# A two-layer hybrid trunk step: scale loaded ahead of shift, decay rows by transposes, lighter vector work in mixer C

## Chip, cores and metric

The kernel runs on one core of one Trainium2 chip. The metric is the device time of one execution in microseconds; a kernel's time is the median of its runs. TensorE is the matrix engine (PE in the rows, with PEld for its weight loads), VectorE is DVE, ScalarE is ACT, GpSimd is POOL, and SP is the queue that issues all transfers here.

## What is computed

Two token streams, 128 context tokens and 256 latent tokens (384 columns together), pass through two layers of model width 1024. A layer first modulates a normalised input, mixes it in three ways side by side, merges the three, and then runs an MLP with squared ReLU. Cut to what matters here:

```python
def residual_block(x, mod, p, mixer):
    sh1, sc1, g1, sh2, sc2, g2 = jnp.split(mod, 6, axis=-1)
    y, extra = mixer(rmsnorm(x, p['norm1_g']) * (1 + sc1) + sh1)
    ...

# mixer C, per direction, head and chunk (gated delta rule)
gc = jnp.cumsum(gl, axis=-1)
decay = exp(gc[:, None] - gc[None, :]) where i >= j, else 0
a_mat = strict_lower((k * beta) @ k.T * decay)
t_mat = inverse(I + a_mat)
o = rmsnorm(o_forward + o_backward, c_onorm_g) * silu(c_z)
```

## The kernel before

Activations are held transposed: a tile is 128 channels by 384 tokens, eight tiles make the model width. A projection is made in three matmuls per 128x128 weight block (high weights by high and by low activations, low weights by high activations; `mm3`, L149 to L152), after a weight tile of 512 KB has been loaded into one of three `raw` buffers and split by ScalarE (high half, L146) and VectorE (low half, L147). The order of the instructions on each engine is chosen when the kernel is built, by a list scheduler that goes by priorities (`phase`, `stream`): the code is written as a "chain" and a "fill" that is worked in beside it, and the order doesn't change while the kernel runs.

Layer 0 begins with `lead()` (from L353). It computes the first two sixths of the modulation, shift and scale, from 8 MB of `w_ada`, in three parts (`PARTS`): part 0 loads the columns of both shift and scale for model blocks 0 to 3 as eight loads of 512 KB, parts 1 and 2 the columns for two blocks each as eight loads of 256 KB. In each part TensorE multiplies the conditioning vectors (the stationary operand, 32 columns wide, in four column groups) by the loaded columns (L155 with tile `mraw`), VectorE transposes the result and adds the bias (L400 to L404), and `modulated` (L217 to L230) makes the tiles hh and hl from `x`, scale, shift and the reciprocal norm `rb`. Between the parts, `advance` runs the projections of w_small and of three key tiles of w_in as far as hh and hl exist: the early projections, whose results wait in PSUM banks. From their banks mixer C's gates (tile `kab`, L556 to L560) and the convolution of the keys (L644 to L659) are made.

In layer 1 the modulation is ready beforehand. There w_small and two key tiles are projected from tiles that are only scaled (`scaled`, L232 to L244, the shift as two more columns), while the norm is computed; `normalised` (L546 to L554) then multiplies the result by the norm and adds the shift's two columns as a bias. All eight tiles of `modulated` are made ahead of it in the code.

Mixer C's chain: for each of three token tiles n and two directions d, the decay rows (tile `gr`, L811 to L833) are twelve bf16 matmuls in which a column of one of three pieces of the log decay, spread over 128 columns, multiplies a triangle of ones (`tri16`); a masking matmul `bar` is added (L825) and ScalarE takes the exponential. VectorE makes the matrices M and QK from them, then inverts the 32x32 diagonal blocks in 31 steps (L866 to L871), transposes the result (L873, L875), and `spread` (L940 to L946) writes it as block-diagonal tiles X0T and X0, four products with the mask `bd2` for each n. Small 64x64 matmuls p1 to p5 finish the inverse; `e1` (L948 to L952) evacuates the first of them, the lower halves on VectorE and the upper ones on ScalarE; `e3` (L959 to L962) applies a correction. Gates of mixer C (`gate`, L710 to L716) are made in the fill: silu(z) times the output gain in a tanh, a pass of VectorE for 0.5 t + 0.5 (L715), and a product with gain and z (L716). The last gating is a plain product (L1097).

## Time and profile before

| | |
|---|---|
| median of 3 runs | 1532.94 us (1529.35 to 1535.46) |
| profiled execution | 1534.62 us, span 1532.8 us |
| mean granted TensorE clock | 0.992 of full |
| TensorE busy | 1490.1 us, 97% of the span, 9694 matmuls |
| VectorE busy | 995.7 us, 65%, 2159 instructions |
| ScalarE busy | 768.6 us, 50%, 1523 instructions |
| moved by DMA | 212.82 MB, mean 139 GB/s |

The profiled execution is one run of its own, so its time differs a little from the median. A matmul's busy time overlaps that of the next one, so the distance from start to start tells what one costs. A wait in the view of the waits is idle time of an engine, put down to what came last.

### The profile page before, as it was taken

The numbers are of one execution on the slowest core, as the hardware profiler recorded it, in microseconds if no ns is written. First come the engines' busy times: TensorE is split into PE (matmuls) and PEld (weight loads), VectorE is DVE, ScalarE is ACT, GpSimd is POOL, SyncE is SP. The second block draws the span as 40 slices with busy tenths as digits, with TensorE's granted clock in tenths as the row PEclk, the third lists the DMA queues.
The fourth block names the chain that finished last, engine by engine and source line by source line (L and its number), as shares of the span: only waits on it lengthen the run. The fifth ranks groups of instructions, "written<-read, shape, count | busy, mean of one in ns | idle before, by whom it ended". The sixth has DMA issues, their size and how long they took to land.

```text
span 1532.8 us, 25235 instructions
## 1 busy us (share of the span) xinstructions
PE 1490.1 (97%) x9694; PEld 1372.9 (90%) x9694; DVE 995.7 (65%) x2159; ACT 768.6 (50%) x1523; POOL 22.4 (1%) x82
## 2 busy tenths in 40 slices
PE   5999999999999999999999999999999999999997
PEld 2898798977889999999998987889889999999997
DVE  4667895564446788888868778956645575553333
ACT  3466634455424666643335576344564456663222
POOL 0000200000000000000000002000000000000000
PEclk9999999999999999999999999999999999999999
DMA  9532131242688466677743331213324434444342
GB/s 316 165 108 86 51 101 56 76 143 89 210 280 270 144 190 197 200 242 241 248 142 113 97 96 54 85 57 106 99 75 138 128 121 124 124 124 127 122 128 77
DMA packets 80856, 212.82 MB, mean 139 GB/s; under 512 B 8800, under 2 KB 24544, under 8 KB 80608
## 3 DMA queue, kind: packets, MB, share of 16 engines
q1 hardware_dynamic: 80736, 211.21, 44.1%
q8 instruction: 76, 1.25, 0.3%
q14 instruction: 44, 0.36, 0.1%
HBM read 204.59 MB, written 4.75 MB: 137 GB/s over the span
## 4 chain that ended last, share of the span: by engine, by line
PE 73%; DVE 10%; issue 10%; DMA 3%; ACT 1%; POOL 1%; SPq 1%; DVEq 0%; POOLq 0%; ACTq 0%
PE g L152 19%; PE g L150 19%; PE g L151 19%; PE c L155 5%; PE f L155 3%; DVE wlo L147 2%; DMA araw<-in_w_ada_dram 2%; PE o L155 2%; DVE aacc L319 2%; PE f L455 1%; PE g L155 1%; DVE h L869 1%; DVE hl L239 1%; DVE blk L871 1%; PE c L150 1%
## 5 line engine op out<-in xcount | busy, mean ns | idle before, releaser
L146 ACT CAST whi<-raw 128x1024 fp32r<-128x1024 f32 x268 | 280.6, 1048 | 479.0 <-PE g L151 429.6
L152 PE MATMUL g<-hh,wlo 128*128 128x384 f32 (+1 forms) x1424 | 487.8, 344 | 6.0 <-DVE wlo L147 6.0
L150 PE MATMUL g<-hh,whi 128*128 128x384 f32 (+1 forms) x1424 | 488.3, 344 | 0.6 <-DVE gpiece L181 0.3
L151 PE MATMUL g<-hl,whi 128*128 128x384 f32 (+1 forms) x1424 | 486.8, 343 | 0.1
L147 DVE TENSOR_TENSOR wlo<-raw,whi 128x1024 fp32r<-128x1024 f32 x268 | 325.9, 1216 | 155.0 <-PE g L152 129.2
L152 PEld LDWEIGHTS g<-hh,wlo 128*128 128x128 f32 x1424 | 269.4, 189 | 15.4 <-DVE wlo L147 10.4
L150 PEld LDWEIGHTS g<-hh,whi 128*128 128x128 f32 x1424 | 269.5, 190 | 9.4 <-issue 6.5
L151 PEld LDWEIGHTS g<-hl,whi 128*128 128x128 f32 x1424 | 269.4, 189 | 6.9 <-issue 3.5
L152 PE MATMUL g<-fh,wlo 128*128 128x384 f32 x512 | 173.0, 338 | 1.0 <-DVE wlo L147 1.0
L150 PE MATMUL g<-fh,whi 128*128 128x384 f32 x512 | 173.4, 339 | 0.0
L151 PE MATMUL g<-fl,whi 128*128 128x384 f32 x512 | 172.6, 337 | 0.0
L319 DVE SCALAR_TENSOR_TENSOR aacc<-araw,cs,aacc 128x512 f32<-128x512 f32 x168 | 117.0, 745 | 13.9 <-DMA araw<-in_w_ada_dram 11.9
L152 PEld LDWEIGHTS g<-fh,wlo 128*128 128x128 f32 x512 | 96.0, 187 | 2.4 <-DVE wlo L147 2.3
L150 PEld LDWEIGHTS g<-fh,whi 128*128 128x128 f32 x512 | 96.0, 188 | 1.6 <-issue 1.6
L151 PEld LDWEIGHTS g<-fl,whi 128*128 128x128 f32 x512 | 96.0, 188 | 0.0
L150 PE MATMUL g<-brh,whi 128*128 128x384 f32 x192 | 65.9, 343 | 0.5 <-DVE gate L537 0.5
L436 ACT ACTIVATE at_p<-at_p,at_nm 128x384 f32<-128x384 f32 (+1 forms) x96 | 51.8, 541 | 28.8 <-DVE at_nm L433 27.8
L152 PE MATMUL g<-brh,wlo 128*128 128x384 f32 x192 | 65.9, 343 | 0.0
L151 PE MATMUL g<-brl,whi 128*128 128x384 f32 x192 | 65.1, 339 | 0.0
L147 DVE TENSOR_TENSOR fl<-fa,fh 128x384 fp32r<-128x384 f32 x64 | 35.5, 555 | 38.9 <-ACT fh L146 38.9
L347 DVE SCALAR_TENSOR_TENSOR x<-g,mod,x 128x128 f32<-128x128 f32 x64 | 23.7, 412 | 51.2 <-PE g L152 47.9
L1231 ACT ACTIVATE fa<-fa,fb 128x128 f32<-128x128 f32 (+1 forms) x128 | 51.1, 447 | 1.9 <-DVE fa L1229 1.9
(333 smaller groups left out, 1885.4 us busy)
## 6 DMA issues: line engine op xcount, KB each, us to landing
raw<-in_w_ff_dram SPq DMA_DIRECT2D x128, 512.0 KB, 3.8
raw<-in_w_in_dram SPq DMA_DIRECT2D x102, 512.0 KB, 3.6
araw<-in_w_ada_dram SPq DMA_DIRECT2D x96, 256.0 KB, 3.4
raw<-in_w_branch_dram SPq DMA_DIRECT2D x24, 512.0 KB, 3.7
araw<-in_w_ada_dram SPq DMA_DIRECT2D x24, 512.0 KB, 6.5
raw<-in_w_out_dram SPq DMA_DIRECT2D x16, 512.0 KB, 3.6
mraw<-in_w_ada_dram SPq DMA_DIRECT2D x8, 512.0 KB, 9.0
mraw<-in_w_ada_dram SPq DMA_DIRECT2D x16, 256.0 KB, 7.2
```

What stands on the lines that cost most here:

```text
L146: S.copy(hi, src)
L147: V.tensor_tensor(out=lo, in0=src, in1=hi.bitcast(F32), op=ALU.subtract)
L150: PE.matmul(ps, lhsT=wh, rhs=rh, start=start, stop=False)
L151: PE.matmul(ps, lhsT=wh, rhs=rl, start=False, stop=False)
L152: PE.matmul(ps, lhsT=wl, rhs=rh, start=False, stop=stop)
L155: return PE.matmul(ps, lhsT=lhsT, rhs=rhs, start=start, stop=stop)
L239: V.scalar_tensor_tensor(out=lo[:, c], in0=x[k][:, c], scalar=gp[:, k, s:s + 1], in1=hi[:, c].bitcast(F32), op0=ALU.mult, op1=ALU.subtract)
L319: V.scalar_tensor_tensor(out=acc[:, s, :], in0=raw, scalar=cs[:, k, s:s + 1], in1=acc[:, s, :], op0=ALU.mult, op1=ALU.add)
L347: V.scalar_tensor_tensor(out=x[k][:, c], in0=ps[:, c], scalar=m[:, b0 + k, s:s + 1], in1=x[k][:, c], op0=ALU.mult, op1=ALU.add)
L436: S.activation(sm[:, :nk], sm[:, :nk], AF.Exp, bias=nm[:, u:u + 1], scale=-1.0, accum_out=den[:, u:u + 1])
L455: PE.transpose(pt[:, j * P:(j + 1) * P], ps_[half, n][:, c * P:(c + 1) * P], ident)
L1231: S.activation(a[:, c], a[:, c], AF.Relu, bias=b[:, s:s + 1])
```

## The change

In layer 0, `lead()` loads `w_ada` in four parts of eight 256 KB loads: scale for blocks 0 to 3, scale for blocks 4 to 7, then shift in the same two halves. The early projections (now w_small and all four key tiles) use tiles that are only scaled, without norm and shift. When the shift is complete, a pass of TensorE with the shift as the stationary operand goes over all early weights and gives their bias (`shifted`, tile ebs); `normalised` multiplies by the norm and adds the bias. The tiles hh and hl for everything else are made from x times scale times norm (tile lt) plus shift. From part 1 on, a part's blocks begin with its last block row. Twelve staging buffers `mraw` serve all parts. In layer 1 kab is normalised after five of the eight modulated tiles. The decay rows become four f32 transposes of the cumulated decay. The gate keeps (t + 1) z, with the factor 0.5 and the gain moved to later steps. `spread` makes X0 on ScalarE, and `e1` copies on ScalarE alone.

```diff
-PARTS = ((4, 2), (2, 1), (2, 1))
+LOADS = (2, 1, 2, 0)
 ...
+    def scaled_tile(k, gp, hi, lo):
+        for s, c in STREAMS:
+            S.activation(hi[:, c], x[k][:, c], AF.Copy, scale=gp[:, k, s:s + 1])
+            V.scalar_tensor_tensor(out=lo[:, c], in0=x[k][:, c], scalar=gp[:, k, s:s + 1],
+                                   in1=hi[:, c].bitcast(F32), op0=ALU.mult, op1=ALU.subtract)
+
+    def normalised(t, ps, b, rb):
+        V.tensor_tensor(out=t, in0=ps, in1=rb[:ps.shape[0]], op=ALU.mult)
+        for s, c in STREAMS:
+            S.activation(t[:, c], t[:, c], AF.Identity, bias=b[:, s:s + 1], scale=1.0)
+        return t
 ...
     def lead():
+        banks = [*twin(), bank(po, "o"), mk(pg, [P, 512], "g"), mk(pg, [P, 512], "g")]
 ...
-        b0 = 0
-        for nb, nw in PARTS:
+        for part, nw in enumerate(LOADS):
             for _ in range(nw):
                 load()
+            b0 = (8, 12, 0, 4)[part]
             ps = bank()
+            raws = []
             for k in range(KT):
-                raw = mk(lp, [P, n * P], f"mraw{nb}", bufs=KT)
-                nc.sync.dma_start(raw.rearrange("p (s c) -> p s c", s=2),
-                                  A["w_ada"][0, k * P:(k + 1) * P, 0:2048].rearrange("p (s c) -> p s c", s=2)[:, :, b0 * P:b1 * P])
+                raws.append(mk(lp, [P, 512], "mraw", bufs=12))
+                nc.sync.dma_start(raws[k], A["w_ada"][0, k * P:(k + 1) * P, b0 * P:(b0 + 4) * P])
 ...
+            else:
+                first = block(KT - 1, 0, True, False)
+                with tc.issue_after(first.ins):
+                    for g in range(1, 4):
+                        block(KT - 1, g, True, False)
+                    for k in range(KT - 1):
+                        for g in range(4):
+                            block(k, g, False, k == KT - 2)
 ...
+            if part < 2:
 ...
+                for k in range(k0, k0 + 4):
+                    hi, lo = mk(lp, [P, T], "lxh", F32R, bufs=KT), mk(lp, [P, T], "lxl", F32R, bufs=KT)
+                    scaled_tile(k, gp1, hi, lo)
+                    xh.append(hi)
+                    xl.append(lo)
+                advance(k0 + 4)
+            if part == 1:
+                ts = [mk(lp, [P, T], "lt", bufs=KT) for _ in range(KT)]
 ...
+            if part == 2:
+                advance(KT)
+
+        V.tensor_copy(sh[:, :, 0:2], mod0[:, 0:KT, :])
+        ps = bank()
+        def shifted(k, w, g, start, stop):
+            return mm(ps[32 * g:32 * g + 32, :160].rearrange("p (t i) -> p t i", i=32), sh[:, k, :],
+                      w[:, k, :, 32 * g:32 * g + 32].bitcast(F32), start=start, stop=stop)
+        first = shifted(KT - 1, wh, 0, True, False)
+        with tc.issue_after(first.ins):
+            for g in range(1, 4):
+                shifted(KT - 1, wh, g, True, False)
+            for k in range(KT):
+                for w in (wh, wl)[k == KT - 1:]:
+                    for g in range(4):
+                        shifted(k, w, g, False, k == KT - 1)
 ...
+        kab = normalised(mk(sp, [48, T], "kab", bufs=1), early.pop(0), ebs[:48, 0, :], rb)
 ...
-            hh, hl = modulated(rb, gp1, mod0, 0)
 ...
+            hh, hl = modulated(rb, gp1, mod0, 0, range(5))
+            for b, ps in zip(ebs, pss):
+                V.tensor_copy(b, ps[:, T:])
+            kab = normalised(mk(sp, [48, T], "kab", bufs=1), early.pop(0), ebs.pop(0), rbs)
+            for out, more in zip((hh, hl), modulated(rb, gp1, mod0, 0, range(5, KT))):
+                out += more
 ...
-                V.tensor_scalar(out=zg, in0=zg, scalar1=0.5, scalar2=0.5, op0=ALU.mult, op1=ALU.add)
-                V.scalar_tensor_tensor(out=zg, in0=zg, scalar=pl[:, Q_ON:Q_ON + 1], in1=ps, op0=ALU.mult, op1=ALU.mult)
+                V.scalar_tensor_tensor(out=zg, in0=zg, scalar=1.0, in1=ps, op0=ALU.add, op1=ALU.mult)
 ...
-                    for i in range(3):
-                        mm(gr[:, h * P:(h + 1) * P], g16[i][:, j:j + 1].to_broadcast([P, P]), tri16[:, d, :],
-                           start=h + i == 0, stop=h + i == 5)
+                    PE.matmul(gr[:, h * P:(h + 1) * P], lhsT=gc[:, d, n, h:h + 1].to_broadcast([P, P]), rhs=ident, start=h == 0,
+                              stop=h == 3, is_transpose=True)
 ...
-                for dst, c in ((X0T[n, d], (Xc, XcT)[d]), (X0[n, d], (XcT, Xc)[d])):
-                    V.tensor_tensor(out=blocks(dst), in0=c[:, u0:u0 + 4, :].unsqueeze(2).to_broadcast([P, 4, 2, 32]),
-                                    in1=bd2.rearrange("p (b c) -> p b c", b=2).unsqueeze(1).to_broadcast([P, 4, 2, 32]),
-                                    op=ALU.mult)
+                V.tensor_tensor(out=blocks(X0T[n, d]), in0=(Xc, XcT)[d][:, u0:u0 + 4, :].unsqueeze(2).to_broadcast([P, 4, 2, 32]),
+                                in1=bd2.rearrange("p (b c) -> p b c", b=2).unsqueeze(1).to_broadcast([P, 4, 2, 32]), op=ALU.mult)
+                for b in range(2):
+                    S.activation(X0[n, d][:, :, 32 * b:32 * b + 32], (XcT, Xc)[d][:, u0:u0 + 4, :], AF.Copy,
+                                 scale=bd2[:, 32 * b:32 * b + 1])
 ...
-                    (S.copy if b else V.tensor_copy)(flat2(WT[n, d][hs]), ps[b][hs, side(d)])
+                    S.copy(flat2(WT[n, d][hs]), ps[b][hs, side(d)])
 ...
-        V.tensor_tensor(out=r, in0=r, in1=rq, op=ALU.mult)
+        V.scalar_tensor_tensor(out=r, in0=r, scalar=0.5, in1=rq, op0=ALU.mult, op1=ALU.mult)
 ...
-                V.tensor_tensor(out=zg[:, c], in0=zg[:, c], in1=osb[n][:, h, :], op=ALU.mult)
+                V.scalar_tensor_tensor(out=zg[:, c], in0=zg[:, c], scalar=pl[:, Q_ON:Q_ON + 1], in1=osb[n][:, h, :],
+                                       op0=ALU.mult, op1=ALU.mult)
```

## Rows read from the trace of the kernel before

**Rows 1.** The page: busy time of each engine; VectorE's busy tenths in 40 slices.
```profile
PE 1490.1 (97%) x9694; PEld 1372.9 (90%) x9694; DVE 995.7 (65%) x2159; ACT 768.6 (50%) x1523; POOL 22.4 (1%) x82
...
DVE  4667895564446788888868778956645575553333
```

**Rows 2.** Waits of TensorE, whole span: us in total, times, longest us.
```profile
PE g L152 <- DVE wlo L147: 7.0, 8, 1.9
PE f L155 <- DVE blk L944: 3.4, 2, 1.7
...
PE f L687 <- ACT tmp L683: 1.8, 1, 1.8
PE c L155 <- DVE g L962: 1.5, 2, 0.8
...
PE c L595 <- ACT kab L553: 0.6, 1, 0.6
```

**Rows 3.** Windows: us, busy of PE, PEld, DVE, ACT, POOL, then PEclk (granted clock).
```profile
27.40:34.20 6.80, 6.16 (x50) 2.78 (x42) 4.11 (x13) 1.71 (x4) 0.00 (x0) 0.50 1.08 359
160.00:187.00 27.00, 25.49 (x186) 20.25 (x184) 25.25 (x72) 15.84 (x45) 10.76 (x38) 1.00 0.07 21
187.80:191.20 3.40, 3.40 (x13) 3.40 (x12) 3.23 (x12) 1.72 (x6) 0.00 (x0) 0.51 0.75 213
228.80:232.20 3.40, 3.40 (x58) 3.20 (x57) 3.20 (x8) 0.37 (x1) 0.00 (x0) 0.50 0.02 5
288.00:300.00 12.00, 11.96 (x76) 11.27 (x75) 8.52 (x30) 2.97 (x6) 0.00 (x0) 1.00 0.25 78
819.30:822.70 3.40, 3.40 (x12) 3.40 (x12) 3.40 (x18) 2.59 (x6) 0.00 (x0) 0.50 0.74 198
990.00:993.40 3.40, 3.17 (x48) 2.89 (x44) 3.08 (x8) 0.94 (x4) 0.00 (x0) 0.50 0.00 0
```

**Rows 4.** Timeline of TensorE in the lead: start us, us, instruction.
```profile
26.50 0.73 PE L150 MATMUL g<-hh,lhi 128*48 128x384 f32 x3
...
39.05 0.86 PE L155 MATMUL c<-mraw,cs 128*32 128x128 f32 x24
39.85 0.38 PE L150 MATMUL g<-hh,lhi 128*48 128x384 f32 x1
...
53.40 0.44 PE L150 MATMUL g<-hh,whi 128*128 128x384 f32 x1
```

**Rows 5.** The same timeline: early projections, the first and the seventh of a run.
```profile
47.77 0.34 PE L150 MATMUL f<-hh,lhi 128*128 128x384 f32 x1
...
48.81 0.34 PE L150 MATMUL g<-hh,lhi 128*48 128x384 f32 x1
```

**Rows 6.** Windows, a stretch of the lead: the last two are DMA share, GB/s.
```profile
16.00:24.00 8.00, 6.45 (x65) 2.21 (x64) 0.30 (x1) 0.48 (x1) 0.00 (x0) 1.00 1.05 391
```

**Rows 7.** The page's DMA issues: count, KB each, us to landing.
```profile
mraw<-in_w_ada_dram SPq DMA_DIRECT2D x16, 256.0 KB, 7.2
```

**Rows 8.** Timeline of TensorE: decay rows in layer 0, and eight f32 transposes.
```profile
173.07 0.84 PE L155 MATMUL c<-tri,gpiece 128*128 128x128 bf16 x12
173.72 0.42 PE L150 MATMUL g<-hh,whi 128*128 128x384 f32 x1
...
293.35 1.06 PE L191 MATMUL c<-cst,rs_y 128*128 128x128 f32 x8
294.16 0.42 PE L150 MATMUL g<-brh,whi 128*128 128x384 f32 x1
```

**Rows 9.** Groups by line and shape: count, busy us, mean ns; one line's view.
```profile
L944 DVE TENSOR_TENSOR blk<-blk,bd 128x256 f32<-128x256 f32 x16 | 8.5, 602 | 0.1
L952 DVE COPY h<-c 64x256 f32<-64x256 f32 x8 | 3.0, 411 | 1.4 <-PE c L155 1.4
L715 DVE TENSOR_SCALAR brz<-brz 128x384 f32<-128x384 f32 x8 | 2.8, 354 | 0.0
...
L952 ACT COPY h<-c x8: 367/367/369, 232.2 to 1005.9; 64x256 f32<-64x256 f32 x8
```

More of the change, by code (lines that the diff above doesn't have):

```diff
@@ L236, in scaled @@
             hi, lo = hidden()
[L237 to L240 removed]
+            scaled_tile(k, gp, hi, lo)
             split(sh[:, sh0 + k, :], hi[:, T:], lo[:, T:])
@@ L377, in load @@
+            split(raw[:, :n].rearrange("p (k c) -> p k c", k=KT), wh[:, :, i, :m], wl[:, :, i, :m])
+            early.append(banks[i][:m, :T])
             at.append(0)
         def advance(k1):
-            for i, (wh, wl) in enumerate(tiles):
+            for i, ps in enumerate(early):
+                m = ps.shape[0]
                 for k in range(at[i], k1):
-                    mm3(early[i], wh[:, k, :], wl[:, k, :], hh[k][:, :T], hl[k][:, :T], k == 0, k == KT - 1)
+                    mm3(ps, wh[:, k, i, :m], wl[:, k, i, :m], xh[k], xl[k], k == 0, k == KT - 1)
@@ new lines, in lead @@
+            if part == 1:
+                ts = [mk(lp, [P, T], "lt", bufs=KT) for _ in range(KT)]
+                for k in range(KT):
+                    for s, c in STREAMS:
+                        V.scalar_tensor_tensor(out=ts[k][:, c], in0=x[k][:, c], scalar=gp1[:, k, s:s + 1], in1=rb[:, c],
+                                               op0=ALU.mult, op1=ALU.mult)
[3 more added lines that the diff above has]
+        ps = bank()
@@ new lines, in lead @@
+        tr = mk(sp, [P, 512], "diag", bufs=1)[:, :160]
+        V.transpose(out=tr, in_=ps[:, :160])
+        ebs = mk(sp, [P, 5, 2], "ebs", bufs=1)
+        tr = tr.rearrange("p (t i) -> p t i", i=32)
+        V.tensor_copy(ebs, tr[:, :, 0:2])
+        kab = normalised(mk(sp, [48, T], "kab", bufs=1), early.pop(0), ebs[:48, 0, :], rb)
+        hh, hl = [], []
+        for k in range(KT):
+            hi, lo = hidden()
+            for s, c in STREAMS:
+                if s == 1 and k % 2 == 1:
+                    V.tensor_scalar(out=hi[:, c], in0=ts[k][:, c], scalar1=mod0[:, k, s:s + 1], scalar2=None, op0=ALU.add)
+                else:
+                    S.activation(hi[:, c], ts[k][:, c], AF.Identity, bias=mod0[:, k, s:s + 1], scale=1.0)
+                V.scalar_tensor_tensor(out=lo[:, c], in0=ts[k][:, c], scalar=mod0[:, k, s:s + 1],
+                                       in1=hi[:, c].bitcast(F32), op0=ALU.add, op1=ALU.subtract)
+            hh.append(hi)
+            hl.append(lo)
@@ L413, in lead @@
         es.close()
-        return hh, hl
+        return hh, hl, rb, kab, [ebs[:, 1 + i, :] for i in range(4)]
     def attend(pool, q, k, vals, mask, scale, sink, oT):
@@ L474, in trunk @@
             xs = load_x(0, A["xT"])
-            hh, hl = lead()
+            hh, hl, rbs, kab, ebs = lead()
         else:
@@ L544, in trunk @@
         es.enter_context(stream("chain"))
-        def normalised(t, ps):
-            M = ps.shape[0]
-            b = mk(sp, [P, 2], "eb")[:M]
-            V.tensor_copy(b, ps[:, T:])
-            V.tensor_tensor(out=t, in0=ps[:, :T], in1=rbs[:M], op=ALU.mult)
-            for s, c in STREAMS:
-                S.activation(t[:, c], t[:, c], AF.Identity, bias=b[:, s:s + 1], scale=1.0)
-            return t
-        ps, kab = early.pop(0), mk(sp, [48, T], "kab", bufs=1)
-        if l == 0:
-            S.copy(kab, ps)
-        else:
-            normalised(kab, ps)
         nc.sync.dma_start(O["krT"][l], kab[0:32, 0:128])
```

67 lines of the change are left out of this document (31 added, 36 removed).

## The prediction

> **What bounds the kernel now.** I read the page first. TensorE has work in 97% of the span and in nine tenths or more of every slice but the first and the last, while VectorE is at eight or nine tenths only in some slices [rows 1]. So this kernel is a queue of TensorE work with few holes, and a change can win only by taking work off TensorE or by closing a hole. The second view is TensorE's waits, which give the holes [rows 2]. 7.0 us are eight waits for the low halves of weights that VectorE had not yet made. 3.4 us are the two waits, one in each layer, for mixer C's spread blocks, 1.5 us the two waits for corrections behind the spread, and 1.8 and 0.6 us are layer 1's value and kab transposes waiting for ScalarE. The third view, the windows, shows what a hole costs after it has closed [rows 3]: right behind each wait of about 2 us stands a stretch of 3.4 us with the granted clock near 0.50 (1.2 GHz in place of 2.4), at 187.8, 228.8, 819.3 and 990 us; one of 6.8 us stands in the lead, from 27.4 us. In 3.4 us at half clock 1.7 us of work is lost, in 6.8 us 3.4 us. The fourth view is the timeline of TensorE in the lead [rows 4]: the first early projection starts at 26.50 us, the first ordinary one at 53.40.
>
> The sum is made against the profiled execution: 1534.62 us with a span of 1532.8. That is 1.7 us above the median of 1532.94, which I take off at the end.
>
> **Prices.** Early projections of 384 columns stand 0.175 us apart (six from 47.77 to 48.81 us) [rows 5]. The w_ada blocks of one k (eight instructions of 128 columns) take 0.27 us: 24 of them from 39.05 to 39.85 [rows 4].
>
> **The lead.** Before, 4.19 MB of w_ada (scale and shift of four blocks) must land ahead of the first projection; after, 2.10 MB. The transfers ran at 391 GB/s [rows 6], so the first projection moves 5.4 us forward, from 26.5 to 21.1 us. What TensorE has to do from there: 120 early products in place of 96, as a fourth key tile comes into the lead (120 x 0.175 = 21.0 us); three parts of blocks in place of two (24 x 0.27 = 6.5); the shift pass, which is new: 16 rounds of four column groups, 160 columns, two passes. No row has it; the nearest is the 128-column block at 0.27. Its ends are 0.27 (four groups side by side, width free) and 0.33 (in proportion to the columns) a round, 4.3 to 5.3 us; I take 5.3, the columns' proportion. Before that pass comes a bridge of VectorE's transpose, bias add and copy, 0.8 us. Sum 33.6 us: the lead would end at 54.7. Before, the same products would be done at 53.4 + 24 x 0.175 = 57.6, and that holds the 3.4 us of the half-clock stretch and 2.4 us of small stalls between blocks and products (26.9 from first early product to first ordinary one, less 96 x 0.175 = 16.8, two parts of blocks 4.3, and 3.4). Of the small stalls I carry half over (1.3): 56.0. With the same half-clock stretch on top the lead loses 1.8 us, with none it gains 1.6; as TensorE now has less of a break ahead of the products I take most of the gain, **1.0 us**, ends -1.8 and (no stalls either) +2.9.
>
> DMA: w_ada goes from 24 loads (8 of 512 KB, 16 of 256 KB) to 32 of 256 KB, and one 512 KB weight load moves from the mixer into the lead; the nine more issues are hidden while the DMA engines are full (share 1.05) [rows 6]. They are not free of waits: twelve staging buffers hold one and a half parts, and each later part's blocks begin with its last block row, so the second half of part 2 can only be issued when part 1's blocks have run, and part 3's when part 2's have. A 256 KB load takes 7.2 us from issue to landing [rows 7]. Cover: part 1's products (48, 8.4 us) and those of the last two key tiles (48, 8.4 us). So it costs nothing while these stand behind the blocks in TensorE's order. VectorE and ScalarE get scaled tiles, shifted tiles and five normalisations more in the lead; VectorE, the busier of the two, stands at four and six tenths in the first two slices [rows 1], so I cost them at nothing; uncovered, the last tile's two operations would hold TensorE by about 1 us, inside the ends above. kab is done some 6 us later than now, covered by projections.
>
> **Decay rows.** Twelve bf16 products per direction and tile occupy TensorE from 173.07 to 173.72, 0.65 us; eight f32 transposes of the same kind as the new ones from 293.35 to 294.16, so four take 0.41 us [rows 8]. 12 groups x 0.24 = **2.9 us** off TensorE. Ends: 0 (VectorE, the slower engine around them, sets the pace there) and 2.9; I take 2.9, since TensorE has 25.5 us of work in the 27 us around them (VectorE 25.3) [rows 3].
>
> **Layer 1's kab ahead of the last three modulated tiles.** The waits of 0.6 and 1.8 us go: kab's two activations leave ScalarE's queue in front of the value copy. Late next is the last modulated tile: 0.7 us (kab's product and the copies of the bias columns) are now ahead of it on VectorE. With the waits goes the half-clock stretch at 819.3 (1.7 us) [rows 3]. 2.4 - 0.7 + 1.7 = **3.4 us**, ends 0 and 4.1.
>
> **Spread, evacuation, gates.** VectorE loses 12 spread products of 0.60 us, 12 copies of 0.41 and 8 gate passes of 0.35 [rows 9]: 15 us, nearly all beside TensorE's work. On the path: tile 2's spread stands right ahead of the corrections that TensorE waits 2 x 0.75 us for, and loses 2 x 0.60 us, so these 1.5 us go. The two waits for the first spread block stay, as the block's own product is the second on VectorE behind the transposes; with one gate pass fewer (0.3 us) in the crowded stretch ahead of it I take 0.6 us for both, and 0.5 us of the wlo waits. Against it: the copies of tiles 0 and 1 now follow each other on ScalarE (0.37 each) instead of going two abreast, 0.5 us a layer. 1.5 + 0.6 + 0.5 - 1.0 = **1.6 us**, ends -2 and +7 (both waits and both half-clock stretches). The new gain multiply on the last gating is a form priced 0.06 us dearer by its neighbours, 24 times, beside merges: nothing; uncovered it would be 1.4 us.
>
> **Sum.** 1.0 + 2.9 + 3.4 + 1.6 = 8.9; 1534.6 - 8.9 = 1525.7, less 1.7: **1524.0 us**.
>
> **A rule against the trace.** The 12 transposes at 293 to 295 us stand in a stretch whose granted clock is 1.00 [rows 3, 8]. The Trainium skill (TensorE: Matmul & The Clock Gate, Part 4: PE-mode transpose) says that transposes do not count as TensorE being busy in the way matmuls do; the trace does not bear that out for short runs between products, and by the rule the sum would be that of the fifth case below.
>
> **The rivals.**
> 1. Forecast, 1524.0, own range 1520 to 1528. Chance 0.48.
> 2. All holes close. If VectorE's relief also removes the two spread waits (3.4 us) and the two half-clock stretches behind them (3.4) and the lead runs at full clock (2.0 more), the time is near 1515. For it: every stretch at 0.50 stands behind a wait. Against: the first spread product cannot start before the 32-wide transposes end. 0.18.
> 3. Time only moves. The instruction order on each engine is laid down when the kernel is built; with other work in it TensorE meets new waits of the old size. Then the decay rows' 2.9 us stay and the rest is nil: 1530.0. For it: VectorE is as full as TensorE around the decay rows [rows 3] and the lead's sum is near nil. 0.26.
> 4. Slower: the staging buffers hold the shift loads back. If TensorE's order puts the shift blocks ahead of the early products, nothing covers the 7.2 us from issue to landing, for part 2 and again for part 3: 14.4 us, and two half-clock stretches of 1.7: 1524.0 + 17.8 = 1541.8. It decides when TensorE reaches the blocks of part 2 or 3 before its last loads were issued 7 us earlier. Against: the code puts 48 products ahead of each. 0.06.
> 5. Slower: the new transposes let the clock fall. If the decay stretch, some 21 us in each layer, ran at half clock, 21 us would be lost: 1545. Against: the row at 288 to 300 us. 0.02.
>
> **The numbers.** 0.5% is 7.7 us, about what a measurement can tell from no change: faster means under 1525.3, slower over 1540.6. Case 1 lies under 1525.3 in three quarters of its chance (0.36) and case 2 wholly (0.18): 0.54. The rest of case 1 and case 3 make the same: 0.38. Cases 4 and 5: 0.08. The range leaves out the slower cases and the outer ends of 2 and 3: 1512 to 1532.
>
> **What would show it.** Right: the first early product near 21 us and the first ordinary projection (with five banks done) near 56 us; decay groups of four transposes at 0.41 us; no wait on the value copy in layer 1 and no half clock near 819 us; the correction waits (1.5 us) gone, the spread waits still there. Wrong: stretches at half clock in new places, a wait of TensorE for w_ada loads after 25 us, or ScalarE's copies as a releaser with over 1 us a layer.

## The result, and the profile after

The changed kernel takes 1542.1 us (median of four runs, 1539.35 to 1545.03). The kernel before took 1531.1 us beside it. The ratio is 1.0067, with a 95% interval of 1.0048 to 1.0086: slower by 10.3 us (7 to 13). The forecast was 1524.0 us.

The profiled execution took 1539.35 us with a span of 1537.6. It lies 2.8 us under its median, and the profiled execution of before 3.5 us over the median of the runs made since, so the two traces show only 4.7 of the 10.3 us. Executions of one kernel mostly lie within some 3 us of their median, single ones up to 8 us away; therefore every experiment below is judged by its ratio, and a ratio of 0.001 is 1.5 us.

First the view of TensorE's waits after (in total, times, longest), which answers to [rows 2]:

```profile
PE g L152 <- DVE wlo L147: 6.4, 7, 3.2
PE g L150 <- DVE lp L679: 4.8, 1, 4.8
PE f L155 <- DVE blk L1003: 3.6, 2, 1.8
...
PE f L750 <- ACT tmp L746: 2.0, 1, 2.0
PE f L150 <- ACT lxh L352: 1.7, 1, 1.7
PE g L150 <- ACT whi L146: 1.6, 1, 1.6
PE c L155 <- ACT h L1013: 0.9, 2, 0.5
```

The waits for the corrections (1.5 us) and for kab (0.6) are gone. In place of the former stand two of 0.45 us for ScalarE's copies (last line), near the 0.5 us a layer that the forecast had for them. The spread waits and the wait for the value copy stand as before. The wlo waits come to the same total, but one is now 3.2 us long, and a single wait of 4.8 us is new. The windows tell where the clock fell (busy of PE, PEld, DVE, ACT, POOL, then the granted clock), and answer to [rows 3]:

```profile
22.70:26.10 3.40, 3.40 (x12) 2.35 (x11) 3.40 (x9) 2.03 (x5) 0.00 (x0) 0.50 1.04 406
60.50:65.50 5.00, 0.29 (x2) 0.00 (x0) 4.62 (x20) 3.26 (x10) 0.00 (x0) 0.81 0.54 162
63.60:70.40 6.80, 4.85 (x15) 4.58 (x16) 6.80 (x30) 4.20 (x10) 0.00 (x0) 0.50 0.22 78
160.00:187.00 27.00, 26.31 (x177) 21.31 (x177) 22.75 (x62) 18.97 (x52) 6.39 (x24) 1.00 0.15 44
...
309.40:316.20 6.80, 6.16 (x24) 5.68 (x23) 5.31 (x13) 2.77 (x5) 0.00 (x0) 0.50 0.58 193
806.00:830.00 24.00, 21.85 (x126) 20.18 (x124) 22.75 (x76) 16.51 (x37) 0.00 (x0) 1.00 0.42 122
1067.20:1070.60 3.40, 3.40 (x12) 3.40 (x12) 1.86 (x5) 0.00 (x0) 0.00 (x0) 0.51 0.76 227
```

Two stretches of 6.8 us at half clock are new. The one at 63.6 us begins within the new wait of 4.8 us, so TensorE has work in only 4.85 us of it; the one at 309.4 us stands behind the wait of 3.2 us. Shorter ones of 3.4 us are new at 1067.2 and 1528.0 us. The ones at 187.8 and 819.3 us are gone, and the one in the lead, 6.8 us before, is 3.4 us long.

**The stall at 60 us.** TensorE's timeline behind the lead (start, us, instruction, idle time before it and its releaser):

```profile
21.53 0.38 PE L150 MATMUL f<-lxh,lhi 128*48 128x384 f32 x1 [1.69 <-ACT lxh L352]
...
50.78 0.44 PE L150 MATMUL g<-hh,whi 128*128 128x384 f32 x1
...
53.10 0.75 PE L155 MATMUL c<-lhi,lsh 128*32 128x160 f32 x16
...
57.58 0.45 PE L150 MATMUL g<-hh,whi 128*128 128x384 f32 x1
...
60.46 0.33 PE L152 MATMUL g<-hh,wlo 128*128 128x384 f32 x1
65.55 0.66 PE L150 MATMUL g<-hh,whi 128*128 128x384 f32 x1 [4.76 <-DVE lp L679]
```

The first early product runs at 21.53 us, the shift pass from 53.10 to 57.58, and 2.3 us of the first ordinary projection stand ahead of it (50.78 to 53.10). So the lead itself is done at 57.58 - 2.32 = 55.3 us, where before the same products would have been done at 57.6. Then TensorE finishes one projection and stands idle for 4.8 us. VectorE's timeline shows why:

```profile
58.18 0.55 DVE L358 TENSOR_TENSOR g<-f,sqacc 128x384 f32<-128x384 f32 x1
...
63.50 0.55 DVE L358 TENSOR_TENSOR g<-o,sqacc 128x384 f32<-128x384 f32 x1
...
64.96 0.44 DVE L248 STREAM_SHUFFLE rp_b<-g 128x256 f32<-128x256 f32 x1
...
67.63 0.56 DVE L358 TENSOR_TENSOR g<-g,sqacc 128x384 f32<-128x384 f32 x1
...
69.26 0.55 DVE L358 TENSOR_TENSOR g<-g,sqacc 128x384 f32<-128x384 f32 x1
```

Projections take their result buffers from three g buffers in rotation. Two of them were given to the lead's last two key tiles (`banks` ends with them), and L358, the normalisation that frees such a buffer, reaches them at 67.63 and 69.26 us, behind the chain of small steps for the decay (lp) and the first key's convolution. The third holds the finished projection until L248, its last reader, is done at 65.40. TensorE goes on 0.15 us later. The releaser that the view names, lp, is only what came last by the profile. The Trainium skill (Perfetto Trace Analysis, Optimization Strategy) says that consistent bubbles, the same gap repeating on an engine that should be saturated, can mean that there is no room for the next tile. Here a single gap meant it.

**The stall at 305 us.** VectorE's timeline at mixer C's last gating, where TensorE waits for a low half of weights (wlo):

```profile
299.86 0.35 DVE L1158 SCALAR_TENSOR_TENSOR brz<-brz,prm,g 128x128 f32<-128x128 f32 x1
...
300.77 2.97 DVE L1158 SCALAR_TENSOR_TENSOR brz<-brz,prm,g 128x128 f32<-128x128 f32 x11
303.65 0.56 DVE L147 TENSOR_TENSOR brl<-brz,brh 128x384 fp32r<-128x384 f32 x1
304.12 0.55 DVE L615 SCALAR_TENSOR_TENSOR y<-gate,g 128x384 f32<-128x384 f32 x1
...
307.21 1.22 DVE L147 TENSOR_TENSOR wlo<-raw,whi 128x1024 fp32r<-128x1024 f32 x1
```

The gating is in the new, dearer form, and the wlo behind it starts only at 307.21 us, twelve instructions and 3.5 us after the gating's end (300.77 + 2.97).

### The profile page after: what moved, and what is told of

It is laid out like the page before. It is cut to its first block, busy times and chain, and to the rows that moved or that the text cites. A ratio compares the mean times of both kernels' runs of the same rounds, so it can differ in the third digit from the quotient of the medians.

```text
span 1537.6 us, 25504 instructions
## 1 busy us (share of the span) xinstructions
PE 1492.1 (97%) x9790; PEld 1382.5 (90%) x9790; DVE 994.9 (65%) x2159; ACT 789.6 (51%) x1580; POOL 22.4 (1%) x82
## 4 chain that ended last, share of the span: by engine, by line
PE 87%; DVE 10%; issue 1%; ACT 1%; DMA 1%; SPq 0%; DVEq 0%; ACTq 0%
PE g L150 22%; PE g L152 22%; PE g L151 22%; PE c L155 6%; PE f L155 3%; PE o L155 2%; DVE wlo L147 2%; PE f L524 2%; PE g L155 2%; DVE blk L931 1%; DVE h L929 1%; PE c L150 1%; DVE hl L353 1%; PE c L152 1%; PE c L151 1%
```

## The experiments

All ratios are to the kernel before on the same chip; the us are (ratio - 1) x 1531.

| kernel | median us | ratio (95% interval) | us |
|---|---|---|---|
| the change | 1542.1 | 1.0067 (1.0048 to 1.0086) | +10.3 |
| change, lead's buffers reordered | 1533.3 | 1.0016 (1.0007 to 1.0025) | +2.4 |
| change, old gates | 1536.2 | 1.0032 (1.0020 to 1.0043) | +4.9 |
| change, both | 1530.1 | 1.0001 (0.9987 to 1.0014) | +0.2 |
| change, no output gain | 1536.0 | 1.0035 (1.0024 to 1.0046) | +5.4 |
| change, no bias in the lead | 1540.6 | 1.0062 (1.0044 to 1.0080) | +9.5 |
| before, lead and layer 1's order | 1539.4 | 1.0055 (1.0043 to 1.0067) | +8.4 |
| the same, buffers reordered | 1537.3 | 1.0041 (1.0026 to 1.0055) | +6.3 |
| change with both, no shift pass | 1528.6 | 0.9980 (0.9969 to 0.9991) | -3.1 |
| change with both, pass twice | 1536.2 | 1.0026 (1.0014 to 1.0039) | +4.0 |
| before, gates alone | 1537.6 | 1.0043 (1.0029 to 1.0057) | +6.6 |
| before, all mixer C parts | 1532.2 | 1.0009 (0.9998 to 1.0021) | +1.4 |
| before, decay rows alone | 1529.9 | 1.0002 (0.9993 to 1.0010) | +0.3 |
| before, spread and evacuation alone | 1530.9 | 1.0003 (0.9991 to 1.0015) | +0.5 |
| before, layer 1's order alone | 1528.2 | 0.9980 (0.9971 to 0.9989) | -3.1 |
| before, tiles moved by 32 bytes | 1528.2 | 0.9986 (0.9973 to 0.9999) | -2.1 |
| before, all but lead and gates | 1525.5 | 0.9970 (0.9959 to 0.9981) | -4.6 |
| the same, light gate, gain on ScalarE | 1524.0 | 0.9954 (0.9936 to 0.9971) | -7.0 |
| the last one, tiles aligned | 1526.5 | 0.9967 (0.9954 to 0.9980) | -5.1 |

Four of these kernels don't compute the whole step: they leave out the output gain, the bias or the shift pass, or count the pass twice. They serve for their times alone.

### The lead's buffers

```diff
-        banks = [*twin(), bank(po, "o"), mk(pg, [P, 512], "g"), mk(pg, [P, 512], "g")]
+        banks = [mk(pg, [P, 512], "g"), mk(pg, [P, 512], "g"), bank(po, "o"), *twin()]
```

> The changed kernel with one line other: the lead's two buffers of the projections' rotation go to the products that are finished first (kab and the first key tile) and not to the last two key tiles. Theory (buffers): the 4.9 us wait for a free buffer behind the second ordinary projection, at 60.5 us, and the 3.4 us lost at half clock behind it go; 1542.1 - 8.3 = 1533.8 us. Rival (order): the wait comes from VectorE being behind with the first gating whatever the buffers are; a wait of 3 to 5 us stays within 10 us of the same place and the time is 1540 to 1544.

Measured: 1533.3 us, as the theory had it. The wait at 60 us and its half clock are gone. In their place stands one wait of 1.3 us, twenty microseconds later, with a stretch of 6.8 us at half clock from 80.7 us:

```profile
71.80 0.44 PE L152 MATMUL g<-hh,wlo 128*128 128x384 f32 x1 [0.51 <-DVE wlo L147]
80.76 1.44 PE L155 MATMUL c<-cst,g 128*128 128x1 f32 x6 [1.27 <-ACT g L824]
```

That the number fits is partly luck. The second stall, ahead of 308.48 us in the changed kernel, is gone here too, although the gates are the change's. On VectorE the low half now follows 0.4 us behind the last gating, and TensorE keeps the full clock there:

```profile
294.33 2.97 DVE L1158 SCALAR_TENSOR_TENSOR brz<-brz,prm,g 128x128 f32<-128x128 f32 x11
...
297.69 1.21 DVE L147 TENSOR_TENSOR wlo<-raw,whi 128x1024 fp32r<-128x1024 f32 x1
```

```profile
300.00:320.00 20.00, 19.36 (x123) 17.67 (x122) 17.11 (x45) 8.48 (x16) 0.00 (x0) 1.00 0.63 197
```

So the 7.8 us between the two kernels (1.0067 to 1.0016) hold the end of both stalls, less what the new wait and its half clock take back.

Was it the buffers' order, or that all normalisations wait for the pass? A kernel in which they need not wait:

```diff
-        V.tensor_copy(ebs, tr[:, :, 0:2])
+        V.memset(ebs, 0.0)
```

> The changed kernel with the bias of the five early projections left out (zeros in place of the pass's result; the pass itself still runs), so that nothing waits for the pass. Theory (lateness: every normalisation of the lead stands behind the pass at 58 us, and the first decay rows' work and the buffers with it): the wait at 60.5 us and its half clock go, 8.3 us, and the smaller waits behind it too, 1531 to 1533 us. Rival (the buffers' order alone: the two in rotation belong to the key tiles that are normalised last): a wait of 3 us or more stays within 10 us of 60 us, 1537 to 1542 us.

The rival holds: 1540.6 us. TensorE still stands for 4.2 us ahead of 66.47 us (its releaser now a piece of the decay), and VectorE's timeline shows the two buffers in rotation freed last again, although nothing holds them back but VectorE's own order:

```profile
66.32 0.55 DVE L358 TENSOR_TENSOR g<-g,sqacc 128x384 f32<-128x384 f32 x1
...
67.95 0.55 DVE L358 TENSOR_TENSOR g<-g,sqacc 128x384 f32<-128x384 f32 x1
```

The edit did not bring kab forward by much (its transposes start at 58.13 us, 59.02 in the changed kernel), so it tests the waiting of the key tiles, not an earlier kab.

### The lead without the rest

All mixer C parts of the change are taken back, the last six places of its diff, of which two stand here:

```diff
-                V.tensor_tensor(out=blocks(X0T[n, d]), in0=(Xc, XcT)[d][:, u0:u0 + 4, :].unsqueeze(2).to_broadcast([P, 4, 2, 32]),
...
+                for dst, c in ((X0T[n, d], (Xc, XcT)[d]), (X0[n, d], (XcT, Xc)[d])):
...
-                    S.copy(flat2(WT[n, d][hs]), ps[b][hs, side(d)])
+                    (S.copy if b else V.tensor_copy)(flat2(WT[n, d][hs]), ps[b][hs, side(d)])
```

> The kernel before with the new lead and layer 1's kab order alone; decay rows, gates, spread and evacuation as before. Theory (buffers): the lead's first part gains 2 us, the wait behind the second ordinary projection and its half clock cost 8.3, layer 1's order gains 3.4: 1531.1 + 2.9 = 1534.0 us. Rival (all of the loss is in mixer C): the lead and layer 1's kab bring what was forecast, 1.0 + 3.4: 1526.7 us.

1539.4 us, 5 us more than even the theory had; the same 4.8 us wait, and 11.5 us over the kernel with layer 1's order alone (1.0055 - 0.9980). With the buffers' line edited as above:

> The kernel before with the new lead and layer 1's kab order alone, and the lead's buffers in the other order. Theory (the buffers carry most of the lead's loss of 11.2 us, and what is left is the pass): 1539.4 less the 6.1 to 8.8 us that the other order was worth with the rest of the change = 1530.6 to 1533.3 us, 2.4 to 5.1 over the kernel before with layer 1's order alone (1528.2). Rival (the order of the buffers matters only with the other parts): 1537 us or more.

1537.3 us: the rival. The stall at 60 us is gone (TensorE reaches the first decay mask at 157.5 us in place of 167.1), and most of what it gave is lost again at 204 to 214 us, where TensorE has transposes and products of attention weights and nothing between them:

```profile
204.97 0.49 PE L524 MATMUL f<-cst,at_p 128*128 128x128 f32 x3
206.14 0.55 PE L524 MATMUL f<-cst,at_p 128*128 128x128 f32 x3 [0.68 <-ACT at_pT L526]
207.46 0.66 PE L524 MATMUL f<-cst,at_p 128*128 128x128 f32 x4 [0.78 <-DVE at_pT L526]
208.79 0.55 PE L524 MATMUL f<-cst,at_p 128*128 128x128 f32 x3 [0.68 <-ACT at_pT L526]
210.06 2.14 PE L155 MATMUL o<-at_pT,vA 128*64 128x128 f32 x12 [0.72 <-DVE at_pT L526]
...
214.03 0.44 PE L150 MATMUL g<-brh,whi 128*128 128x384 f32 x1 [0.98 <-ACT brh L146]
```

Five of these waits make 3.8 us (0.68 + 0.78 + 0.68 + 0.72 + 0.98), with a half-clock stretch of 3.4 us among them. Projections are what covers such chains, and their number is fixed: my reading is that those used up early are missing here, which no run tested by itself.

### The shift pass

Both runs start from the change with the buffers reordered and the old gates, 1.0001.

```diff
-        first = shifted(KT - 1, wh, 0, True, False)
-        with tc.issue_after(first.ins):
...
+            for w in (wl, wh):
+                for k in range(KT):
+                    for g in range(4):
+                        shifted(k, w, g, False, w is wh and k == KT - 1)
```

The first of the two runs takes the lines with - away, the second adds the lines with + behind them.

> The changed kernel with the lead's buffers in the other order and the gates as before, and without the shift pass: the bias of the five early projections is taken from the shift tile as it stands, so they lack the right shift. Theory (what the mended lead still costs, 1530.1 - 1525.5 = 4.6 us, is the pass): 1530.1 - 4.4 = 1525.7 us. Rival (it is VectorE's and ScalarE's work, which comes behind the lead in a heap whatever the pass does): 1529 us or more.

> The changed kernel with the lead's buffers in the other order and the gates as before, and the shift pass run twice over (the bias of the five early projections is doubled). Theory (the pass counts in full): 1530.1 + 4.4 = 1534.5 us. Rival (TensorE has time to spare there, as it waits for VectorE's chain behind the lead): 1530 to 1532 us.

Without the pass the kernel is 3.2 us faster (1.0001 to 0.9980), with two passes 3.8 us slower, each within some 3 us. The trace has 4.5 us of TensorE time for one (53.10 to 57.58 us). So it counts for the most part, and the second run's rival falls. The first run lies between its two numbers: TensorE still waits 1.3 us ahead of 71.8 and 1.5 us ahead of 76.9 us, both times for ScalarE, and has 10.2 us at half clock from 73.9 us.

### The gates

```diff
-                V.scalar_tensor_tensor(out=zg, in0=zg, scalar=1.0, in1=ps, op0=ALU.add, op1=ALU.mult)
+                V.tensor_scalar(out=zg, in0=zg, scalar1=0.5, scalar2=0.5, op0=ALU.mult, op1=ALU.add)
+                V.scalar_tensor_tensor(out=zg, in0=zg, scalar=pl[:, Q_ON:Q_ON + 1], in1=ps, op0=ALU.mult, op1=ALU.mult)
...
-                V.scalar_tensor_tensor(out=zg[:, c], in0=zg[:, c], scalar=pl[:, Q_ON:Q_ON + 1], in1=osb[n][:, h, :],
-                                       op0=ALU.mult, op1=ALU.mult)
+                V.tensor_tensor(out=zg[:, c], in0=zg[:, c], in1=osb[n][:, h, :], op=ALU.mult)
```

> The changed kernel with the gates as they were before: the factor 0.5 and the gain in two passes on the early gate, a plain product on the last gating. Theory (late gain): the waits for low halves of weights at the start of mixer B go (3.4 and 0.7 us in layer 0, 1.7 and 1.2 in layer 1, 7.0 together) and with them the half-clock stretches at 309 and 1067 us (3.4 and 1.7 us of work lost): 1542.1 - 12.1 = 1530.0 us. Rival (crowding ahead): the waits come from where the low-half subtraction stands in VectorE's order, which the other parts set; they stay at 2 us or more a layer, and the two passes put back cost up to 3 us more in the earlier stretch: 1540 to 1545.

1536.2 us: 5.4 us by the ratios, about half of what the theory gave, as a wait of 2.1 us for a high half of weights (whi) and 3.4 us of half clock at 315.5 us appear in the place of the old ones. Which of the two edited places does it? The last of them alone:

> The changed kernel with the output gain left out of mixer C's last gating (a plain product there, as before; the lighter early gate stays), so the output lacks that gain. Theory (the dearer form on the last gating makes VectorE late with the low half that TensorE waits for): the time of the kernel with the gates wholly as before, 1536.2 us, and no wait over 1 us for a low half at mixer B's start. Rival (the early gate's missing pass, or the order of the engines that comes with it, does it): 1542 us with the 3.4 us wait still there.

1536.0 us, the theory's number, in a kernel that lacks the gain. With the plain product VectorE's timeline at the same place reads:

```profile
302.56 2.31 DVE L1158 TENSOR_TENSOR brz<-brz,g 128x128 f32<-128x128 f32 x11
304.78 1.22 DVE L147 TENSOR_TENSOR wlo<-raw,whi 128x1024 fp32r<-128x1024 f32 x1
305.92 0.55 DVE L615 SCALAR_TENSOR_TENSOR y<-gate,g 128x384 f32<-128x384 f32 x1
```

Eleven products take 2.31 us in place of 2.97. That is 0.66 us. But the wlo now stands right behind them, where the change has it 3.5 us behind: the order of the engines is laid down when the kernel is built, and in the change the branch's four splits (brl) and other work are put ahead of it. The form costs 0.66 us, the order that comes with it the rest. And the form alone does not decide the order: with the lead's buffers reordered, the same form has the wlo 0.4 us behind it, as shown above.

The gates' three places put into the kernel before, by themselves and then with the other parts of mixer C:

> The kernel before with the gates of the change and nothing else. Theory (the gates cost by themselves what their return was worth in the changed kernel, 5.9 us): 1530.9 + 5.9 = 1536.8 us, with a wait of 2 us or more for a low half near 300 us. Rival (they cost only where the lead has already made mixer C late): 1531 us.

> The kernel before with decay rows, gates, spread and evacuation of the change, and with its own lead and layer 1's kab order. Theory (late gain): 2.9 us less by the decay rows, 1.5 by the corrections' waits, 12.1 more by the waits at the start of mixer B with their half clock: 1531.1 + 7.7 = 1538.8 us. Rival (all of the loss is in the lead): 1531.1 - 2.9 - 1.6 = 1526.6 us.

Alone they cost 6.6 us (1537.6; the theory), with a wait of 3.2 us ahead of 305.8 us. With decay rows, spread and evacuation the same wait of 3.2 us is there, ahead of 299.73 us, and 10.2 us at half clock, yet the kernel is only 1.4 us slower than before: between the theory (+7.7) and the rival (-4.5). So the parts don't simply add: the prices of the gates (6.6), of the decay rows (0.3) and of spread and evacuation (0.5), each taken alone, make 7.4 us. Why stays open.

### Decay rows, spread and evacuation

```diff
-                    for i in range(3):
-                        mm(gr[:, h * P:(h + 1) * P], g16[i][:, j:j + 1].to_broadcast([P, P]), tri16[:, d, :],
-                           start=h + i == 0, stop=h + i == 5)
+                    PE.matmul(gr[:, h * P:(h + 1) * P], lhsT=gc[:, d, n, h:h + 1].to_broadcast([P, P]), rhs=ident, start=h == 0,
+                              stop=h == 3, is_transpose=True)
```

> The kernel before with the decay rows as transposes and nothing else. Theory (TensorE sets the pace there): 12 groups x 0.24 us less: 1531.1 - 2.9 = 1528.2 us. Rival (VectorE and ScalarE set the pace around the decay rows): the 2.9 us turn into waits within 10 us of the rows, 1531.1 us. Third (transposes let the clock fall): stretches at half clock at 160 to 190 and 920 to 945 us, 1545 us.

No difference: +0.3 us (-1.1 to +1.5). Four transposes take 0.35 us to the next start here (172.82 to 173.17 us), even less than forecast. The rows of the changed kernel say nearly the same, 0.36 us:

```profile
172.65 0.60 PE L875 MATMUL c<-cst,gc 128*128 128x128 f32 x4
173.01 0.42 PE L152 MATMUL g<-hh,wlo 128*128 128x384 f32 x1
```

So 12 x (0.65 - 0.36) = 3.5 us of TensorE's time are saved, and not gained. The windows of this kernel suggest why: from the decay rows to the spread VectorE (third pair) has work in 37.4 of 39 us and in 40.4 of 42 us, slightly more than TensorE (37.1 and 40.0), and TensorE waits for it at the end.

```profile
187.00:226.00 39.00, 37.06 (x226) 35.09 (x226) 37.37 (x88) 18.58 (x32) 0.00 (x0) 1.00 0.34 108
...
938.00:980.00 42.00, 39.97 (x243) 37.67 (x241) 40.35 (x94) 20.31 (x36) 0.69 (x2) 1.00 0.34 101
```

In layer 1 the first decay mask starts at 911.26 us and the spread, behind a wait of 1.78 us for VectorE, at 979.74: 68.5 us. Before it was 920.54 to 988.53 with a wait of 1.68: 68.0 us. In all twenty traces this stretch of layer 1 takes 68.0 to 69.5 us, with decay rows of either kind; that VectorE sets this length is my reading. What TensorE saves it spends on other projections (busy 66.4 of these 68.5 us, before 64.3 of 68.0), and those are missing later, where a wait is new:

```profile
1059.01 0.69 PE L150 MATMUL g<-brh,whi 128*128 128x384 f32 x1 [2.05 <-ACT gate L529]
```

```diff
+                for b in range(2):
+                    S.activation(X0[n, d][:, :, 32 * b:32 * b + 32], (XcT, Xc)[d][:, u0:u0 + 4, :], AF.Copy,
+                                 scale=bd2[:, 32 * b:32 * b + 1])
...
-                    (S.copy if b else V.tensor_copy)(flat2(WT[n, d][hs]), ps[b][hs, side(d)])
+                    S.copy(flat2(WT[n, d][hs]), ps[b][hs, side(d)])
```

> The kernel before with the spread and the evacuation of the change and nothing else. Theory (as the sum of the parts leaves it: decay rows, spread and evacuation together brought 2.7 us beside layer 1's order, the decay rows by themselves 0 to 1): 1530.8 - 2.0 = 1528.8 us. Rival (both only make room on VectorE where TensorE does not wait for it): 1530.8 us.

The rival: +0.5 us (-1.4 to +2.3). Beside layer 1's order the three parts together bring 1.5 us (0.9980 to 0.9970), so something of the forecast's 4.5 us is there, within the uncertainty of either run.

### Layer 1's order, and what came with it

```diff
-            hh, hl = modulated(rb, gp1, mod0, 0)
+            hh, hl = modulated(rb, gp1, mod0, 0, range(5))
...
+            kab = normalised(mk(sp, [48, T], "kab", bufs=1), early.pop(0), ebs.pop(0), rbs)
+            for out, more in zip((hh, hl), modulated(rb, gp1, mod0, 0, range(5, KT))):
+                out += more
```

> The kernel before with layer 1's kab normalised after five of the eight modulated tiles, and nothing else. Theory (as forecast, by the time that the changed kernel shows): the waits for kab (0.6 us) and the half clock near 819 us (1.7 us) go, the wait for the value copy stays: 1531.1 - 2.3 = 1528.8 us. Rival (the hole moves): the wait for the value copy brings its half clock back in a neighbouring stretch, 1531.1 us.

3.1 us faster, more than the theory's 2.3. But the profile has its gain in a place that the edit does not touch. In the last feed-forward stage of layer 1 TensorE never waits and the clock is at 1.00; here are 120 us of it, first of this kernel, then of the changed one:

```profile
1390.00:1510.00 120.00, 120.00 (x694) 120.00 (x694) 41.65 (x48) 31.91 (x35) 0.00 (x0) 1.00 0.36 114
```

```profile
1400.00:1520.00 120.00, 120.00 (x681) 120.00 (x680) 41.68 (x48) 32.04 (x35) 0.00 (x0) 1.00 0.37 114
```

694 products against 681: 172.9 ns each against 176.2. The kernel before has 681 too. With the new order three little tiles take 32 bytes more than two did, and every tile placed behind them moves. So only the tiles were moved:

```diff
-            b = mk(sp, [P, 2], "eb")[:M]
+            b = mk(sp, [P, 2], "eb", bufs=3)[:M]
```

> The kernel before with three buffers in place of two for layer 1's little bias tile, and nothing else; this only moves every tile placed behind it by 32 bytes, as layer 1's kab order does in the kernels made from the one before. In the profiles of those the products of the last feed-forward stage of layer 1 (the stage runs for 135.15 us in the kernel before and in the changed one) stand 173.3 ns apart in place of 176.7, the stage takes 132.61 us, and the tiles fh and fl begin at multiples of 128 bytes. Theory (placement): the stage takes 132.6 us here too and 2.5 us of what was put down to layer 1's order (3.1) come with it: 1531.0 - 2.5 = 1528.5 us. Rival (layer 1's order itself): the stage stays at 135.15 us and the time at 1531 us.

The theory: 694 products in the same 120 us, and 2.1 us less (0.2 to 4.1).

```profile
1390.00:1510.00 120.00, 120.00 (x694) 120.00 (x694) 42.89 (x49) 34.05 (x37) 0.00 (x0) 1.00 0.39 122
```

By the medians of the ratios two thirds of the 3.1 us are the tiles' place, then, and 1.0 us is left for the order, which is within the uncertainty: the wait for kab is gone, the one for the value copy (2.0 us) is not. In the changed kernel, which has other small tiles, the stage stays slow (681); what it lost by that, 2.1 us, is in the figures for the lead, which compare kernels of either kind.

### Sums, and a faster kernel

First the change with the buffers' line and the gates' three places edited as above:

> The changed kernel with both edits: the lead's buffers in the other order, and the gates as before. Theory (two separate losses, which add): 1533.3 less the 5.9 us that the gates' return was worth by itself = 1527.4 us. Rival (one loss hides the other, as the later part waits less when it comes earlier or the order of the engines is laid down anew): 1531 to 1535 us.

1530.1 us, 0.2 us over the kernel before: between the two. The gates count 2.3 us here (1.0016 to 1.0001, within the uncertainty), where they cost 5.4 in the change itself: the stall that they bring there was already gone.

The kernel before with the edits above for decay rows, spread, evacuation and layer 1's order:

> The kernel before with the decay rows, spread and evacuation of the change and with layer 1's kab order; its own lead and its own gates. Theory (the parts without the lead and the gates bring what was forecast, about): the same four parts with the gates measured 1532.2; less 5.9 for the gates and 2.6 for layer 1's order (the stretch from layer 1's first projection to the first decay row in the changed kernel against the one before) = 1523.7 us. Rival (only the decay rows count): 1531.1 - 2.9 = 1528.2 us.

1525.5 us, 4.6 us faster than before, between the two numbers and nearer to the theory's. Then the light gate with the gain in another place, on ScalarE, right behind the early gate:

```diff
+                S.activation(zg, zg, AF.Copy, scale=pl[:, Q_ON:Q_ON + 1])
```

> The kernel before with decay rows, spread, evacuation and layer 1's kab order of the change, the lighter early gate too, and the gain as a pass of ScalarE right behind the early gate, so that the last gating is the plain product. Theory (the gain was in the wrong place, the lighter gate itself does no harm): 1525.5 us as with the old gates, or up to 1 us less. Rival (the early gate's lighter form itself changes the order at mixer B's start): 1529 us or more.

1524.0 us, ratio 0.9954: 7.0 us faster than before and 17 faster than the change, the best of all runs. The theory holds; the 2.4 us between the two kernels are within the uncertainty, and a wait of 2.7 us for a high half of weights (whi) ahead of 309.34 us remains. Some 2 us of what either kernel gains is the tiles' place: both run the last feed-forward stage the faster way (694 products in 120 us in the second). Last, the same kernel with tiles aligned (the core of the edit):

```diff
-        return mk(hp, [P, T + 2], "hh", F32R, bufs=KT), mk(hp, [P, T + 2], "hl", F32R, bufs=KT)
+        t = mk(hp, [P, 784], "hh", F32R, bufs=KT)
+        o = 16 * (len(pairs) % 2)
+        pairs.append(t)
+        return (t[:, :T + 2], t[:, 392:394 + T]) if wide else (t[:, o:o + T], t[:, o + T:o + 2 * T])
```

> The kernel before with decay rows, spread, evacuation, layer 1's kab order and the lighter gate with the gain on ScalarE, and with the tiles hh and hl of the mixers and all weight tiles begun at multiples of 128 bytes (hh and hl of one block share a tile). Theory (placement counts for every product that reads such a tile): some 2700 projection products of 384 columns stand 173.3 ns apart in place of 176: 1524.0 - 7.3 = 1516.7 us. Rival (placement of the moving tiles matters in the last stage alone, where nothing else is in the way; in the mixers the waits set the time): 1522 to 1524 us.

1526.5 us, 0.9967, no faster; from 90 to 150 us TensorE ran 368 products, 369 without the alignment. The theory falls, and the time is over the rival's 1522 to 1524 us too: 128 bytes are not the rule for every product, and what the rule is stays open.

## Why the prediction was wrong

| part | forecast, us | measured, us |
|---|---|---|
| lead | -1.0 (-2.9 to +1.8) | +7.4 in the change (9.5 with the tiles' place) |
| decay rows | -2.9 (-2.9 to 0) | +0.3 alone |
| layer 1's order | -3.4 (-4.1 to 0) | -1.0 (-3.1 with the tiles' place) |
| spread, evacuation | -1.6 with the gates (-7 to +2) | +0.5 alone, -1.5 with the decay rows |
| gates' late gain | 0 (0 to 1.4) | +5.4 in the change, +2.3 with the buffers reordered, +6.6 alone |

Step by step along the kernels: layer 1's order -1.0, the three parts of mixer C -1.5 (0.9980 to 0.9970), the lead +7.4 (0.9970 to 1.0032 is 9.5, less 2.1), the gates +5.4 (1.0032 to 1.0067), together +10.3. That sum closes by its making; the independent prices differ, as 11.5 for the lead (9.4 without the tiles' place) beside layer 1's order alone.

**The lead: the step "kab is done some 6 us later than now, covered by projections" failed.** The terms up to it held: first product at 21.5 us (forecast 21.1), pass 4.5 us (I took 5.3, the lower end was 4.3), end of the lead at 55.3 us (56.0). That the end fits is partly luck: the pass (by 0.8 us) and the three parts of blocks (1.9 us each in place of 2.2) were shorter than taken, and a stretch at half clock from 22.7 to 26.1 us (1.7 us of work lost), where I had taken almost none, used that up. But I costed VectorE's and ScalarE's work behind the pass at nothing, uncovered at about 1 us, and never asked who holds the result buffers. A projection can cover only while it has a buffer to write to. Before, the lead's buffers in rotation belonged to kab and the first keys, which were read first; in the change they belong to the two key tiles that are read last. In the trace that cost 4.8 us of standing and 2.4 us by the half clock, as TensorE had work in 4.85 us of that stretch. By the ratios the other order of the buffers brings 7.8 us in the change, which includes the end of the second stall, 4.7 with the old gates, and 2.1 where all of mixer C is as before and the loss comes back later. The pass itself counts 3 to 4 us, which I had set against the earlier start.

**The gates: "beside merges: nothing; uncovered it would be 1.4 us" failed.** The price was right (2.97 against 2.31 us for eleven), the place was wrong: the last gating is not beside merges but ahead of the low half that TensorE reads next. What it cost came through the order that was built around it, 3.2 us of waiting in layer 0 and the half clock behind; where the order came out otherwise, with the buffers reordered, the same form brings no such wait.

**The decay rows: of the ends 0 and 2.9 the wrong one was taken.** I read the window of 27 us around the rows, where TensorE and VectorE are equally full. The stretch that decides runs on to the spread; it keeps its length with shorter decay rows, and VectorE is what TensorE waits for at its end. This is the third case, time that only moves, for this part.

**Layer 1's order** came out at the forecast's size by chance. The wait for kab went; the wait for the value copy, which I had counted in, stayed; two thirds of the gain is the tiles' place. The spread and evacuation brought less than their term too: the waits for the corrections went, but the kernel with these two parts alone is no faster (-1.4 to +2.3 us).

The slower cases that I had named did not come. No wait for `mraw` is in the view of the waits, and a load lands 5.7 us after its issue. The clock is at 1.00 from 160 to 187 us, with the new transposes in it; the rule of the Trainium skill (TensorE: Matmul & The Clock Gate, Part 4: PE-mode transpose) that they do not count as TensorE being busy in the same way showed no effect here. The one that came, a buffer that is freed last, was not among them.

## What to carry to other kernels

Where a first stage hands its results to a loop that rotates buffers, give the rotating ones to the results that are read first, and price every edit that delays a reader by the loop's free buffers, not by how much work stands behind. Where an order is laid down at build time, a dearer form ahead of a wait can cost what the order does with it: look at which instruction comes next on that engine, and put the work on an engine with room, far ahead. And look for the gain of an edit in the stages that it doesn't touch before it is put down to the edit.

## What the runs showed of the hardware

Moving tiles by 32 bytes changed the distance of products in a stage without waits at full clock from 176.2 to 172.9 ns, and the kernel by 2.1 us (0.2 to 4.1); aligning other tiles likewise did nothing. And the same wait for the value copy has different costs: 2.0 us with the clock at 1.00 from 806 to 830 us of the changed kernel, and 1.99 us, followed by 3.4 us at half clock, in the kernel with layer 1's order alone:

```profile
812.80:816.20 3.40, 3.40 (x13) 3.40 (x12) 3.40 (x18) 3.05 (x7) 0.00 (x0) 0.50 0.89 284
```

The kernel before had shown it as well: behind its wait of 1.87 us ahead of 949.43 us the clock stays at 1.00, so half clock does not stand behind every wait of about 2 us, as I had read it.

```profile
949.43 0.45 PE L152 MATMUL g<-hh,wlo 128*128 128x384 f32 x1 [1.87 <-DVE wlo L147]
```

```profile
945.00:957.00 12.00, 10.13 (x62) 9.45 (x61) 11.66 (x32) 8.43 (x19) 1.72 (x5) 1.00 0.34 98
```

So a half-clock stretch can't be booked to a wait of 2 us as a fixed price, as I did for layer 1's order.
